# Layer norm with residual on one core: a transfer list of 24 entries in DRAM blocks of 64 rows, in place of 31 entries in blocks of 16

## The chip, the cores and the metric

The kernel runs on one core of a Trainium2 chip. The metric is device time in microseconds (us) of the whole program; lower is better. An ordinary execution and one taken with the profiler differ little. "Span" is the stretch from the first to the last instruction in a profile, some 1.3 us shorter than the device time of the same execution (236.7 against 238.0). Faster or slower needs 2%. A run counts as fast when it lies within 1.5% of the fastest of its kernel. In the views DVE is VectorE, ACT is ScalarE, POOL is GpSimd and SP is SyncE, which issues the transfers; a `q` after a name means the part of the engine that reads its instructions.

## The reference, cut to what matters

```python
# x, residual: (16, 1024, 512) float32; gamma = ones(512), beta = zeros(512)
z = x + residual
mean, var = z.mean(-1), z.var(-1)
out = gamma * (z - mean) / sqrt(var + eps) + beta
```

The 16384 rows of 2048 bytes are spread over 128 partitions, so each partition handles 128 rows of x, of the residual and of the output. Everything is moved once: 67.1 MB in and 33.6 MB out.

## The kernel before: the parts that matter

One list drives all large transfers. A word such as `x16+16` means: load rows 16 to 31 of every partition; `r` is the residual, `o` a store of the result. From here on a "row" is one row in each of the 128 partitions.

```python
BLOCK = 16
Z_ROWS = 64          # x, later the result: room for 64 rows per partition
R_ROWS = 32          # residual, later the sum: room for 32
PLAN = """
x0+8 r0+8 x8+8 r8+8 x16+16 r16+16 x32+16 r32+16 x48+16
o0+16 r48+16 o16+16 x64+16 r64+16 x80+16 o32+16 r80+16
x96+16 r96+16 o48+8 o56+8 r112+8 x112+8 r120+8 x120+8
o64+16 o80+16 o96+16 o112+8 o120+4 o124+4
"""
```

In DRAM, a partition owns `BLOCK` consecutive rows of each stretch of 128 x `BLOCK` rows. A transfer may not cross a block, and becomes one packet per partition:

```python
def dram(t, lo, n):
    b0 = lo - lo % BLOCK
    v = t[P * b0 : P * (b0 + BLOCK), :].rearrange("(p j) d -> p j d", p=P)
    return v[:, lo - b0 : lo - b0 + n, :].rearrange("p a b -> p (a b)")
```

SyncE issues the list in order on one queue, and waits only where a buffer must be free or a result ready:

```python
for kind, lo, n in moves:
    if kind == "x":       # room in zbuf: the stores of the rows 64 earlier have landed
        ...
        move(part(zbuf, Z_ROWS, lo, n), dram(xf, lo, n), sx[...])
    elif kind == "r":     # room in rbuf: rows 32 earlier have passed the reciprocal
        if lo + n > R_ROWS:
            last = (lo + n - R_ROWS) // TURN - 1
            nc.sync.wait_ge(s_rstd[last % Z_TURNS], last // Z_TURNS + 1)
        move(part(rbuf, R_ROWS, lo, n), dram(rf, lo, n), sr[...])
    else:                 # the results are there
        nc.sync.wait_ge(s_out, lo + n)
        move(dram(of, lo, n), part(zbuf, Z_ROWS, lo, n), so[...])
```

(Cuts are marked by "..."; the last branch omits its test for a wait already made.) The computing runs in turns of 4 rows: GpSimd adds, ScalarE takes mean, square sum and root, VectorE the reciprocal and two multiply-adds.

Of the kernel before, what the change touches and what calls it, by code (L numbers as in the profile page):

```python
# [10 lines left out]
ALU = mybir.AluOpType  # L11


BLOCK = 16
Z_ROWS = 64
R_ROWS = 32


PLAN = """
x0+8 r0+8 x8+8 r8+8 x16+16 r16+16 x32+16 r32+16 x48+16  # L20
o0+16 r48+16 o16+16 x64+16 r64+16 x80+16 o32+16 r80+16
x96+16 r96+16 o48+8 o56+8 r112+8 x112+8 r120+8 x120+8
o64+16 o80+16 o96+16 o112+8 o120+4 o124+4
"""


# [12 lines left out]
def kernel(  # L39
# [23 lines left out]
    for word in PLAN.split():  # L63
        kind, (lo, n) = word[0], map(int, word[1:].split("+"))
        assert lo // BLOCK == (lo + n - 1) // BLOCK
        moves.append((kind, lo, n))
# [6 lines left out]
# [5 lines that stand above are left out]
# [235 lines left out]
```

## Time and profile before

| what | number |
|---|---|
| time, three runs | 239.14 us median (238.11 to 239.16) |
| span of the profiled execution | 236.7 us |
| packets of the data queue | 4464 = 31 x 128 data packets + 31 x 16 semaphore writes |
| busy: VectorE, ScalarE, GpSimd | 75%, 78%, 61% |

The page's table of DMA issues shows the sizes. Each line has what is moved, the issuing queue, the count, KB of one transfer and the median us from issue to landing.

```profile
zbuf<-in_x_dram SPq DMA_DIRECT2D x6, 4096.0 KB, 28.9
rbuf<-in_residual_dram SPq DMA_DIRECT2D x6, 4096.0 KB, 21.2
out_dram<-zbuf SPq DMA_DIRECT2D x6, 4096.0 KB, 31.0
...
out_dram<-zbuf SPq DMA_DIRECT2D x2, 1024.0 KB, 10.0
```

A 4096 KB transfer keeps 16 engines for 9.7 us (8 packets of 1213 ns each); here 21 to 31 us pass to its landing. The difference is time spent queued behind others, the sign of a queue that is kept full.

### The profile page before, as it was taken

How to read it: one execution, taken by the hardware profiler on the slowest of the kernel's cores; microseconds unless marked ns; L12 is line 12 of the kernel's file. 1: busy time of each engine (PE TensorE's matmuls, PEld its weight loads, DVE VectorE, ACT ScalarE, POOL GpSimd, SP SyncE). 2: the span in 40 equal slices, each digit the busy share in tenths (PEclk: the TensorE clock that was granted, in tenths of full speed). 3: DMA queues.
4: the chain of work that ended last, by engine and by line, in shares of the span. 5: the costliest groups of instructions: out<-in, count | busy, mean ns of one | idle time of the engine just before them, and what ended most of it. 6: DMA issues, size and time to landing. Idle time of an engine off the chain costs nothing.

```text
span 236.7 us, 1000 instructions
## 1 busy us (share of the span) xinstructions
PE 3.8 (2%) x4; PEld 1.2 (0%) x4; DVE 177.2 (75%) x290; ACT 183.8 (78%) x545; POOL 144.0 (61%) x36
## 2 busy tenths in 40 slices
PE   0600000000000000000000000000000000000000
PEld 0100000000000000000000000000000000000000
DVE  0001999629999999599980999809999999999950
ACT  2019997299999996999909998099999999999600
POOL 0098920999799307993079920899799798800000
DMA  8999999999999999999999999999999999999997
GB/s 310 443 426 432 426 443 443 443 443 443 410 388 443 443 443 432 426 393 432 443 443 443 443 438 421 415 421 432 429 424 435 426 432 440 439 432 443 438 390 324
DMA packets 4469, 100.68 MB, mean 425 GB/s; under 512 B 498, under 2 KB 498, under 8 KB 500
## 3 DMA queue, kind: packets, MB, share of 16 engines
q1 hardware_dynamic: 4464, 100.67, 99.4%
q14 instruction: 1, 0.01, 0.0%
q10 hardware_dynamic: 4, 0.00, 0.0%
HBM read 67.11 MB, written 33.55 MB: 425 GB/s over the span
## 4 chain that ended last, share of the span: by engine, by line
ACT 48%; DMA 35%; POOL 6%; DVE 4%; issue 1%; SPq 1%; ACTq 0%; DVEq 0%; POOLq 0%
DMA rbuf<-in_residual_dram 35%; ACT junk_s L211 25%; ACT junk_m L201 21%; POOL rbuf L178 6%; DVE zbuf L239 3%; ACT std L220 2%; DVE zbuf L253 1%; SPq L140 1%; DVE rstd L247 0%; ACTq L194 0%; DVEq L231 0%; POOLq L175 0%; ACTq L199 0%; ACTq L195 0%
## 5 line engine op out<-in xcount | busy, mean ns | idle before, releaser
L178 POOL TENSOR_TENSOR rbuf<-zbuf,rbuf 128x2048 f32<-128x2048 f32 x32 | 143.7, 4521 | 62.2 <-DMA rbuf<-in_residual_dram 60.0
L239 DVE SCALAR_TENSOR_TENSOR zbuf<-rbuf,nm,gamma_p 128x512 f32<-128x512 f32 x128 | 87.1, 743 | 47.8 <-ACT std L220 47.8
L201 ACT ACTIVATE junk_m<-rbuf 128x512 f32<-128x512 f32 x128 | 74.2, 580 | 34.0 <-POOL rbuf L178 33.7
L211 ACT ACTIVATE junk_s<-rbuf,nm 128x512 f32<-128x512 f32 x128 | 88.8, 694 | 1.0
L253 DVE SCALAR_TENSOR_TENSOR zbuf<-zbuf,rstd,beta_p 128x512 f32<-128x512 f32 x128 | 87.1, 744 | 1.1
L211 ACT ACTIVATION_READ_ACCUMULATOR junk_s<-rbuf,nm 128x1 f32 x128 | 23.9, 187 | 0.0
L201 ACT ACTIVATION_READ_ACCUMULATOR junk_m<-rbuf 128x1 f32 x128 | 23.8, 186 | 0.0
L220 ACT ACTIVATE std<-ssq,eps_t 128x4 f32<-128x4 f32 x32 | 9.5, 297 | 1.0
L247 DVE RECIPROCAL rstd<-std 128x4 f32<-128x4 f32 x32 | 5.5, 171 | 0.0
L192 ACT ACT_TABLE_LOAD x1 | 1.3, 1283 | 2.7 <-PEq L60 2.7
L131 PE MATMUL gamma_p<-gb_row,ones 1*128 1x512 f32 x2 | 2.0, 1122 | 6.6 <-DMA gb_row<-in_gamma_dram 6.6
L131 PE MATMUL beta_p<-gb_row,ones 1*128 1x512 f32 x2 | 1.9, 1056 | 0.0
L126 DVE MEMSET ones<- 1x128 f32 x1 | 0.2, 165 | 2.0 <-PEq L60 2.0
L131 PEld LDWEIGHTS beta_p<-gb_row,ones 1*128 1x128 f32 x2 | 0.7, 332 | 1.0 <-DMA gb_row<-in_beta_dram 0.5
L131 PEld LDWEIGHTS gamma_p<-gb_row,ones 1*128 1x128 f32 x2 | 0.5, 306 | 6.6 <-issue 6.6
L294 POOL MEMSET const-float32-0.0<- 128x1 f32 x1 | 0.1, 98 | 0.2 <-issue 0.2
L294 POOL MEMSET const-bfloat16-1.0<- 128x1 bf16 x1 | 0.1, 101 | 0.0
L294 POOL MEMSET const-uint8-127<- 128x1 uint8 x1 | 0.1, 101 | 0.0
L294 POOL MEMSET const-float32-1.0<- 128x1 f32 x1 | 0.1, 98 | 0.0
L127 DVE MEMSET eps_t<- 128x1 f32 x1 | 0.1, 59 | 0.0
## 6 DMA issues: line engine op xcount, KB each, us to landing
zbuf<-in_x_dram SPq DMA_DIRECT2D x6, 4096.0 KB, 28.9
rbuf<-in_residual_dram SPq DMA_DIRECT2D x6, 4096.0 KB, 21.2
out_dram<-zbuf SPq DMA_DIRECT2D x6, 4096.0 KB, 31.0
zbuf<-in_x_dram SPq DMA_DIRECT2D x4, 2048.0 KB, 14.9
rbuf<-in_residual_dram SPq DMA_DIRECT2D x4, 2048.0 KB, 14.0
out_dram<-zbuf SPq DMA_DIRECT2D x3, 2048.0 KB, 22.5
out_dram<-zbuf SPq DMA_DIRECT2D x2, 1024.0 KB, 10.0
gb_row<-in_gamma_dram ACTq DMA_DIRECT2D x1, 2.0 KB
```

What stands on the lines that cost most here:

```text
L126: nc.vector.memset(ones[:, :], 1.0).then_inc(s_const, 1)
L131: nc.tensor.matmul(dest[:, :], ones[:, :], gb_row[:, k * D : (k + 1) * D], start=True, stop=True).then_inc(s_pe, 1)
L140: i = nc.sync.dma_start(out=out, in_=in_).then_inc(s, 16)
L178: nc.gpsimd.tensor_tensor(out=z, in0=part(zbuf, Z_ROWS, lo, n), in1=z, op=ALU.add).then_inc(s_sum[lo // TURN % R_TURNS], 1)
L192: act.preload_act_table_set("sqrt_and_others")
L201: i = act.activation(out=junk_m[k][:, :], in_=part(rbuf, R_ROWS, r, 1), func=ACT.Identity, scale=-inv_d, accum_out=column(nm, r),)
L211: i = act.activation(out=junk_s[k][:, :], in_=part(rbuf, R_ROWS, r, 1), func=ACT.Square, bias=column(nm, r), accum_out=column(ssq, r),)
L220: act.activation(out=column(std, rows[0], TURN), in_=column(ssq, rows[0], TURN), func=ACT.Sqrt, bias=eps_t[:, 0:1], scale=inv_d,).then_inc ...
L239: dve.scalar_tensor_tensor(out=part(zbuf, Z_ROWS, r, 1), in0=part(rbuf, R_ROWS, r, 1), scalar=column(nm, r), in1=gamma_p[:, :], op0=ALU.ad ...
L247: dve.reciprocal(out=column(rstd, rows[0], TURN), in_=column(std, rows[0], TURN)).then_inc(s_rstd[j], 1)
L253: i = dve.scalar_tensor_tensor(out=z, in0=z, scalar=column(rstd, r), in1=beta_p[:, :], op0=ALU.mult, op1=ALU.add,)
L294: nc = _bacc.Bacc("TRN2", target_bir_lowering=False, num_devices=1)
```

## The change

Its intent: pay the fixed cost of a transfer fewer times. Blocks of 64 rows allow transfers of more than 16 rows (the longest in the list has 28), and the order was chosen with a model of the queue so that it should not run dry.

```diff
-BLOCK = 16
+BLOCK = 64
 PLAN = """
-x0+8 r0+8 x8+8 r8+8 x16+16 r16+16 x32+16 r32+16 x48+16
-o0+16 r48+16 o16+16 x64+16 r64+16 x80+16 o32+16 r80+16
-x96+16 r96+16 o48+8 o56+8 r112+8 x112+8 r120+8 x120+8
-o64+16 o80+16 o96+16 o112+8 o120+4 o124+4
+x0+16 r0+8 r8+24 x16+20 x36+28 r32+16 o0+16 o16+8
+r48+16 x64+24 r64+16 o24+24 r80+16 x88+16 r96+12 o48+16
+x104+8 r108+8 x112+16 r116+12 o64+16 o80+24 o104+16 o120+8
 """
```

No instruction of a computing engine is added, removed or reordered.

## The prediction

> **What bounds the kernel now.** I read the page's rows by slices of time first, then the DMA table, then the queue's own waits, then the chain of waits, and last the transfer records of the trace.
>
> ```profile
> DVE  0001999629999999599980999809999999999950
> ACT  2019997299999996999909998099999999999600
> DMA  8999999999999999999999999999999999999997
> GB/s 310 443 426 432 426 443 443 443 443 443 410 388 443 443 443 432 426 393 432 443 443 443 443 438 421 415 421 432 429 424 435 426 432 440 439 432 443 438 390 324
> ...
> q1 hardware_dynamic: 4464, 100.67, 99.4%
> ```
>
> The DMA row is 9 in 38 of 40 slices, with 8 at the start and 7 at the end. The table says the same: the packets of the one data queue fill 99.4% of the time of all 16 engines. VectorE and ScalarE have visible holes (75% and 78% busy), so neither is full.
>
> The chain of waits seems to contradict this: it gives ACT 48% and DMA 35%.
>
> ```profile
> ACT 48%; DMA 35%; POOL 6%; DVE 4%; issue 1%; SPq 1%; ACTq 0%; DVEq 0%; POOLq 0%
> ```
>
> That chain follows the last store back through the wait that allowed it to be issued. It can't see that the store, once issued, stands behind others in the queue. The queue's own waits show how early the issuing engine runs:
>
> ```profile
> SPq L140 <- DVE rstd L247: 131.6, 7, 38.5
> SPq L140 <- DVE zbuf L253: 50.6, 7, 22.9
> SPq L140 <- DMA out_dram<-zbuf: 32.9, 4, 17.9
> ...
> SPq L164 <- DMA out_dram<-zbuf: 5.5, 2, 3.1
> ```
>
> The issuer waits 215 us at line 140 for buffers and results, yet the DMA engines are never empty: each wait ends while earlier transfers still lie in the queue. So the ScalarE part of the chain is slack, and the end is set by **the sum of the packet times**. In the stretches the view by windows agrees:
>
> ```profile
> 64.00:72.00 8.00, 0.00 (x0) 0.00 (x0) 7.77 (x14) 7.71 (x25) 8.00 (x3) 1.00 0.97 397
> 72.00:180.00 108.00, 0.00 (x0) 0.00 (x0) 89.28 (x146) 92.11 (x275) 72.63 (x17) 1.00 1.00 431
> 180.00:228.00 48.00, 0.00 (x0) 0.00 (x0) 46.03 (x75) 42.12 (x126) 24.16 (x6) 1.00 1.00 431
> ```
>
> The last two columns are DMA share and GB/s: full share at 431 GB/s, through loads, mixtures and pure stores alike.
>
> The records of single packets give the size of that sum. The quickest of each size (and nearly the median): 8192 B 309 ns, 16384 B 611 ns, 32768 B 1213 ns, a 4-byte semaphore write 9 ns. From the last two sizes, 16384 B cost 602 ns, so a row of 2048 B costs 75.25 ns, and 611 - 602 = **9 ns are fixed per packet**. A transfer has one packet per partition, 8 for each of 16 engines, and one semaphore write per engine. So n rows hold every engine for 8 x (75.25 n + 9) + 9 ns = 0.602 n + 0.081 us. For 384 rows (128 of x, 128 of residual, 128 out) in 31 transfers: 231.2 + 31 x 0.081 = 233.7 us. What packets took beyond their quickest adds 1.5 us per engine: 0.7 in the first 4 us, 0.4 around 68 to 72 us (each engine had one slow packet there, up to 1908 ns in place of 1213), the rest scattered. Total 235.2, against 235.16 us of summed packet time per engine in the trace. The remaining 1.5 us of the span of 236.7 are the 1.0 us before the first packet and about 0.5 at the end, where engines stop between 234.9 and 236.1.
>
> **What the Trainium skill says.** Four places, all in "DMA: Bandwidth & Descriptors". "Where 436 GB/s comes from" puts the ceiling at 435 GB/s; the trace agrees: 16 x 2048 B / 75.25 ns = 435.5 GB/s without the fixed part. "Why small descriptors are slow (HBM only)" names a fixed overhead per packet that large ones amortize; this trace shows 9 ns, 0.7% of a 32 KB packet. "Rules for kernel authors" wants at least 1 MiB per DMA; the smallest here is already 1024 KB. "Latency and other measured facts" reports that row pitches in HBM at large powers of two cost bandwidth: 512 KiB gives 207 GB/s per direction where 214 is full, 2 MiB gives 164. The trace of before has only a 32 KiB pitch and shows no loss.
>
> **The change, part by part.**
>
> (1) Fewer transfers. 31 become 24: 7 x 8 = 56 packets fewer per engine at 9 ns = 0.50 us, and 7 semaphore writes at 9 ns = 0.06 us. Sum: **0.57 us** of engine time, all on the path that sets the end, as all engines are full. The bytes stay: 231.2 us remain untouched. Seven issues fewer at 0.33 to 0.5 us each save 2 to 3 us of the issuing engine, which stands waiting most of the time: worth 0.
>
> (2) Block 64. A partition's rows in DRAM now start 128 KiB apart, not 32 KiB, and one packet can be up to 28 rows = 56 KiB. No instruction is added. If 56 KiB goes out as one packet, its cost is the formula's. If it were split in two, the packets saved would partly return: 9 ns x 8 per split transfer, at most 11 transfers above 16 rows or so, under 0.7 us.
>
> (3) The order. This is worth something only if the queue ran dry before, and it did not. It can only lose, if it runs dry now. I walked the new list with measured durations. A transfer ends 0.602 n + 0.081 us after the one before; the first begins at 1.1 and loses 0.7. Data is usable 1.0 us after its last packet (before: residual rows 16 to 31 end by this rule at 40.8; GpSimd's wait for them ended in the trace at 41.37). Four rows take GpSimd 4.54 us, ScalarE 5.76 us (2.46 + 2.94 + 0.30 and gaps in the chain), VectorE 2.85 us to the reciprocal that frees the residual buffer and 5.56 us to the end. An issue takes 1.0 us to its first packet (0.00 to 1.02 in the trace). The rule gives the old list's waits at 43.2, 72.4, 95.5, 121.0, 150.1 us for residual rows 32, 48, 64, 80, 96; the trace has 42.8, 72.0, 95.3, 120.9, 150.1. So it is good to 0.5 us, on the safe side.
>
> One step in full: residual rows 64 to 79 need rows 32 to 47 to have passed the reciprocal. Those end in the queue at 69.7, are usable at 70.7, the first add ends at 75.4 (0.1 for the wait), four ScalarE turns at 98.4, the reciprocal at 101.3. The queue is filled until 108.6. Spare time: 108.6 - 101.3 - 1.0 = 6.3 us. The gated transfers of the new list:
>
> ```
> transfer   may issue  queue filled to  spare us
> r32+16        51.0        60.0          7.9
> r48+16        74.7        84.3          8.6
> x64+24        85.9        94.0          7.1
> r64+16       101.3       108.6          6.3
> r80+16       125.7       132.8          6.1
> x88+16       134.4       142.5          7.1
> r96+12       144.1       152.2          7.1
> x112+16      170.8       179.0          7.2
> o104+16      213.1       220.3          6.2
> o120+8       224.7       230.0          4.4
> ```
>
> The old list by the same rule never has less than about 6 us ahead of the last stores and 3.9 us before the last one. So both lists keep the queue fed, and part 3 is worth 0. The last store is ready at 224.7, before the queue reaches it: the end stays with the packets.
>
> Sum: 236.7 - 0.6 = **236.1 us of span**, and 239.1 - 0.6 = **238.5 us** of measured time.
>
> **The rivals.**
>
> *The pitch costs bandwidth.* For it: the skill's series starts losing at 512 KiB, and engines that run in step would now touch addresses four times further apart. Against it: 128 KiB is a quarter of the smallest pitch that lost anything, and packet times here are so constant (1213 to 1221 ns for the middle nine tenths) that memory behind them seems to have room. With the 3% of the 512 KiB case on all packets the time would be 231 x 1.03 + 7, about 245 us: slower.
>
> *The queue runs dry.* For it: transfers are larger, so each wait asks for more rows, and the last spare is only 4.4 us. Against it: the walk, which misses the old list by under 1 us. A hole would cost its own length, so even a 2 us error in two places leaves it near 239.
>
> *A real gain above 2%.* It would need 4.8 us. Bytes alone at 75.25 ns a row take 231.2 us, plus 2.5 us outside the span (239.1 - 236.7) and 1.0 us before the first packet: 234.7 us with packets, semaphores, slow start and tail all at zero, still above the 234.4 needed. Only a higher byte rate could bring it, and nothing in the diff gives that.
>
> *Noise hides it.* The three times before span 1.05 us, wider than the gain.
>
> **Range and chances.** The centre is 238.5. Below it lie 0.6 us of run spread and the slow packets that may go away (up to 0.7 us): 237.2. Above it lie the same spread, a split of large packets (0.7) and a mild pitch effect (0.2%, 0.5 us): 240.2. Faster by over 2% has 0.02, slower by over 2% (above 243.9, practically only the pitch) 0.03, same 0.95.
>
> **What the new profile would show.** Step 1: 24 x 128 = 3072 data packets and 384 semaphore writes, 3456 on the queue, the queue's share still over 99%, summed packet time per engine near 234.6. Step 2: 32 KiB packets at 1213 ns and 24 rows at 1815 ns (24 x 75.25 + 9); longer ones would mean the pitch costs, and more packets than 3456 a split. Step 3: no slice of the DMA row under 9 but the first and last; issues of residual rows within 1 us of my table. The prediction is wrong if the packets' time per byte changes, if the queue has holes in the middle, or if the part outside the span moves.

## The result, and the profile after

| | before | after |
|---|---|---|
| median of 6 runs of the same rounds | 238.38 us (238.09 to 239.16) | 238.30 us (238.04 to 238.53) |
| ratio of the fast runs | | 0.9989, 95% interval 0.997 to 1.0009 |
| span of the profiled execution | 236.7 us | 236.9 us |

A ratio here is the mean time of one kernel's fast runs over that of the other's of the same rounds, so it is not quite the ratio of the medians quoted. The change is worth 0.3 us give or take 0.5: the same within 2%, and not distinguishable from nothing.

The rows by slices, and the line of the data queue, of the changed kernel:

```profile
DMA  9999999979999999999999899999999999999997
GB/s 354 399 443 473 456 408 415 508 329 465 443 354 443 393 465 423 490 398 398 443 407 506 382 426 431 422 431 441 409 423 451 425 436 429 479 407 431 437 396 329
...
q1 hardware_dynamic: 3456, 100.66, 99.3%
```

The engines are as full as before: 99.3% after 99.4%. The 7 in slice 9 and the 8 in slice 23 are no holes. The view by windows gives the stretch just before each a DMA share above 1 (slice 9: 1.16, then 0.76, then 1.09; slice 23: 1.02 at 124 to 130 us, 0.90 at 130.3 to 136.2), which fits a packet's time being counted where it starts; by the packets' own records all 16 engines are busy at every instant sampled in both slices. In the run below whose 28-row load is cut in two, slice 9 is a 9 again. GB/s jumps between 329 and 508 for the same reason: packets are now up to 56 KB long.

The chain of waits by engine, and the queue's own waits (engine, line, what for, total us, times, longest; `rstd` is the reciprocal that frees the residual buffer, `zbuf` the finished rows):

```profile
DMA 44%; ACT 36%; POOL 8%; DVE 6%; issue 1%; SPq 0%; DVEq 0%
```

```profile
SPq L139 <- DVE rstd L246: 116.6, 7, 47.3
SPq L139 <- DVE zbuf L252: 65.8, 6, 24.4
SPq L139 <- DMA out_dram<-zbuf: 21.5, 2, 13.2
SPq L147 <- DMA out_dram<-zbuf: 11.8, 1, 11.8
```

The chain moved 12 points from ScalarE to other engines, DMA above all, while the time stayed. That is the reading to learn: where the queue is full, as here, this chain says which of several slack paths happened to be followed, not what sets the end. SyncE still waits over 200 us in total, and the engines never notice.

The issue times are in the timeline of the queue (start us, us, engine, line):

```profile
50.63 0.33 SPq L139 DMA_DIRECT2D rbuf<-in_residual_dram  x1
...
74.25 0.34 SPq L139 DMA_DIRECT2D rbuf<-in_residual_dram  x1
86.47 0.34 SPq L139 DMA_DIRECT2D zbuf<-in_x_dram  x1
101.79 0.33 SPq L139 DMA_DIRECT2D rbuf<-in_residual_dram  x1
...
126.19 0.33 SPq L139 DMA_DIRECT2D rbuf<-in_residual_dram  x1
134.75 0.33 SPq L139 DMA_DIRECT2D zbuf<-in_x_dram  x1
144.88 0.33 SPq L139 DMA_DIRECT2D rbuf<-in_residual_dram  x1
```

The prediction's table had 51.0, 74.7, 85.9, 101.3, 125.7, 134.4 and 144.1: right to 0.8 us. Five of the seven came later than the table, so the rule was not "on the safe side" here; 6 us of spare time covered that.

**Where the saving went.** Two stretches of the changed kernel in the view by windows (stretch, busy us and count of PE, PEld, DVE, ACT, POOL, then clock, DMA share, GB/s):

```profile
64.00:72.00 8.00, 0.00 (x0) 0.00 (x0) 7.61 (x13) 7.28 (x22) 0.72 (x1) 1.00 1.00 385
72.00:180.00 108.00, 0.00 (x0) 0.00 (x0) 95.35 (x156) 99.02 (x296) 84.03 (x19) 1.00 1.00 430
```

From 64 to 72 us the DMA share is 1.00 but only 385 GB/s move (0.97 and 397 before); the stretch after it has 430 (431 before). So something is slow just ahead of 72 us. I took the packets' own records, and for each packet the time above the quickest of its size (9, 309, 611, 912, 1213, 1514, 1815, 2116 ns for 4 B and for 8 to 56 KB in steps of 8). Called "excess" from here on, in us per engine (the sum over all packets / 16):

```
                               records    quickest   excess   sum     of the excess: last load
                               per engine times                       ahead of the first store
before                            279      233.66     1.50    235.16   x48+16  0.45
changed kernel                    216      233.11     2.15    235.26   r32+16  0.91
```

The part that the change was made for is there: 233.66 - 233.11 = 0.55 us. (This column is counts times quickest times, so it shows that counts and quickest times came as expected, not that the time was saved.) The excess took it back, 0.65 us. Most sits where the engines turn from loads to stores: the load packet before last, on all 16 engines at once, lasted up to 2171 ns in place of 1213 (in the old list it is the last one, up to 1908). In the old list one load pays this, x48+16, and hardly any later one. In the new list r32+16 paid twice as much, and three later loads ahead of stores (r64, r96, r116) another 0.17, 0.17 and 0.08.

### The profile page after: what moved, and what is told of

The parts are those of the page before. It is cut to its first block, busy times and chain, and to the rows that moved or that the text cites. A ratio compares the mean times of both kernels' runs of the same rounds, so it can differ in the third digit from the quotient of the medians.

```text
span 236.9 us, 985 instructions
## 1 busy us (share of the span) xinstructions
PE 4.1 (2%) x4; PEld 1.0 (0%) x4; DVE 177.2 (75%) x290; ACT 184.1 (78%) x545; POOL 144.1 (61%) x36
## 3 DMA queue, kind: packets, MB, share of 16 engines
q1 hardware_dynamic: 3456, 100.66, 99.3%
## 4 chain that ended last, share of the span: by engine, by line
DMA 44%; ACT 36%; POOL 8%; DVE 6%; issue 1%; SPq 0%; DVEq 0%
DMA rbuf<-in_residual_dram 26%; ACT junk_s L210 19%; DMA zbuf<-in_x_dram 17%; ACT junk_m L200 16%; POOL rbuf L177 8%; DVE zbuf L238 5%; ACT std L219 2%; DVE zbuf L252 1%; DVE rstd L246 0%; SPq L139 0%; DVEq L230 0%
```

## The experiments

Theories: **P**, the wider pitch in DRAM makes the turns costly; **S**, size and order of the transfers do; **C**, chance of one profile. Apart from these I tested the two premises of the prediction: what a packet really costs, and whether the walk of the queue finds holes. All kernels gave correct results. They ran on four chips (the first four runs on one, the next four on a second, three on a third, the last on a fourth), each round with the kernel before in it; its medians there lay between 238.06 and 238.30 us. Times are compared within rounds; an excess comes from one profile of each altered kernel, two of the unaltered ones, and is compared across chips (that of the first comparison is not on record), so that the chip and the scatter of one profile are not excluded as causes of its differences.

**The pitch alone.**

```diff
 # the kernel before
-BLOCK = 16
+BLOCK = 64
```

> The old list of 31 transfers, only the DRAM block raised from 16 to 64 rows (a partition's rows 128 KiB apart in place of 32). Theory P (the pitch makes the last load packets before a run of stores slow): the time that packets take beyond the quickest of their size rises from 1.5 us per engine to about 2.1, with slow packets ahead of the later store runs too (near 90, 128, 167, 196 us), and the time rises by 0.4 to 0.7 us. Rival S (size and order of the new list do it): 1.5 us as before, time within 0.2 us of the kernel before. Rival C (chance of one run): either, without a pattern at the changes from loads to stores.

Measured: 238.32 us, ratio to before 1.0008 (0.9987 to 1.0029). Excess 1.63 us by the scale above, first turn 0.46, one later turn at 0.16 (r48+16). With the old list the first turn is untouched by the pitch, so the pitch alone does not explain the 0.9 us, and the time shows no cost of 128 KiB. Whether pitch and new list together make the turn slow was not tested.

**Twice the pitch again.**

```diff
 # the changed kernel
-BLOCK = 64
+BLOCK = 128
```

> The new list with the DRAM block raised from 64 to 128 rows (256 KiB apart). Theory P: the excess grows further, from 2.15 to 2.5 us or more per engine, and the time by 0.3 us or more over 238.3. Rivals S and C: 2.1 us and 238.3 us, no change.

Measured: 239.47 us (239.02 to 240.45), ratio to before 1.0056 (1.0033 to 1.0079), an interval clear of the changed kernel's (0.997 to 1.0009). Excess 2.65 us in the profiled run, one of the quicker (239.06), of it 1.33 in r32+16 and 0.28 in r96+12. So a pitch effect exists, some 0.6%, but at 256 KiB and not visibly at 128.

**What a packet costs.** The new list, every entry cut into pieces of 4 rows:

```diff
-x0+16 r0+8 r8+24 x16+20 ...
+x0+4 x4+4 x8+4 x12+4 r0+4 r4+4 r8+4 r12+4 ...        # 96 entries in all
```

> The new list with every transfer cut into pieces of 4 rows: 96 transfers in place of 24, packets of 8 KiB, same order and pitch. 72 more transfers put 576 packets and 72 semaphore writes on each engine. Theory R (the records' 9 ns each are all paid): 648 x 9 ns = 5.8 us more, 244.1 us. Rival O (neighbouring packets of an engine overlap by some 3.3 ns, as their records in the trace do, so only 5.7 ns each are paid): 3.7 us more, 242.0 us. Were nothing of it on the path that sets the end: 238.3 us.

Measured: 242.79 us, ratio to before 1.0189 (1.017 to 1.0208). The page still has a full queue:

```profile
DMA  8999999999999999999999999999999999999996
...
q1 hardware_dynamic: 13824, 100.67, 99.8%
```

Against the changed kernel's 238.30 that is 4.5 us for 648 more records per engine, 6.9 ns each, between the two theories. (By the mean end of the 16 engines, 239.15 against 235.80 and 235.47 in two profiles of the changed kernel, it is 5.4 ns. Against the kernel before, of the same rounds, it is 4.5 us for 585 more records, 7.7 ns.) The excess, 2.70 us, is 0.5 to 0.8 above that of the two profiles of the changed kernel, so part of the 4.5 us is no fixed cost of a record. So the records do cost time on the path that sets the end, but not all of their 9 ns; that neighbouring records of an engine overlap by 3 to 4 ns in the traces fits this. For the change's 63 records fewer this gives an estimate of 63 x 5.4 to 7.7 ns = 0.34 to 0.49 us, not 0.57. A surprise: the first turn cost nothing measurable here, on 8 KB packets on both sides.

**A naive merge.** The old list with neighbours merged where blocks of 16 allow it:

```diff
 # the kernel before; the other words unchanged
-x0+8 r0+8 x8+8 r8+8
+x0+16 r0+16
-o48+8 o56+8 r112+8 x112+8 r120+8 x120+8
+o48+16 r112+16 x112+16
-o112+8 o120+4 o124+4
+o112+8 o120+8
```

> The old list with its 8-row and 4-row neighbours merged to 16 rows wherever the block of 16 allows: 25 transfers, pitch 32 KiB kept. The walk of the queue predicts three holes: 3.5 us before residual rows 32 to 47 (near 50 us), 3.5 us before residual rows 112 to 127 (near 180 us) and 1.3 us before the last store. By the walk the time is 243.3 - 235.5 = 7.8 us above the old kernel less 0 for fewer packets (already in the walk): about 246 us. Rival (the order costs nothing, only the number of packets counts): 0.4 us below the kernel before, 237.9 us.

Measured: 247.98 us, ratio 1.0404 (1.0384 to 1.0424): 25 transfers in place of 31, and 9.6 us slower. The rows of the page, and two stretches in the view by windows (stretch, busy us and count of PE, PEld, DVE, ACT, POOL, then clock, DMA share, GB/s):

```profile
DMA  8999999939999999999999999999949999999988
...
q1 hardware_dynamic: 3600, 100.66, 96.3%
```

```profile
50.00:55.00 5.00, 0.00 (x0) 0.00 (x0) 4.96 (x9) 4.97 (x16) 5.00 (x2) 1.00 0.39 105
...
180.00:188.00 8.00, 0.00 (x0) 0.00 (x0) 7.33 (x13) 7.73 (x24) 8.00 (x3) 1.00 0.51 184
```

The holes are where the walk put them, before residual rows 32 to 47 and 112 to 127. Here the roles are exchanged: ScalarE and GpSimd are full in the stretch and the queue waits for them. The walk said 7.8 us in all. By the packets' records the holes were 3.4, 3.5 and 0.9 us, a little less than its 3.5, 3.5 and 1.3. What it did not have came on top: each restart of the idle queue cost 0.7 us of excess, and the first turn after each restart 0.97 and 1.25 us, together 3.2 us more than the old list's one turn of 0.45. (Holes and restarts sum to 11.0 us; the profiled span is 10.1 longer, 246.8 against 236.7. The 54 records fewer per engine explain at most 0.5 of the difference, the rest is not placed.) So the order is worth nothing only as long as it leaves no hole; this list of fewer transfers in the old layout cost 4%. The new blocks and the searched order reach 24 transfers without a hole; a better order of 25 in blocks of 16 was not tried.

**Does the size of the packets at a turn set its cost?** Three edits of the new list, and the changed kernel unaltered:

```diff
 # last 4 load rows ahead of each run of stores on their own
-r32+16 ... r64+16 ... r96+12 ... r116+12
+r32+12 r44+4 ... r64+12 r76+4 ... r96+8 r104+4 ... r116+8 r124+4
 # first 4 store rows on their own
-o0+16 ... o24+24 ... o48+16 ... o64+16
+o0+4 o4+12 ... o24+4 o28+20 ... o48+4 o52+12 ... o64+4 o68+12
 # the 28-row load cut
-x36+28
+x36+12 x48+16
```

> The new list, but the last 4 rows of each of the four loads that stand ahead of a run of stores are a transfer of their own (r32, r64, r96, r116), so that the engines turn from loads to stores on 8 KiB packets; 28 transfers. Theory L (what costs at a change is the load packet in flight, in proportion to its size): the excess of those loads falls from 1.33 us in sum to 0.4 or less; 4 more transfers cost 0.3 us; time 237.7 us. Rival T (the change costs what it costs, whatever the size of the last load): 1.33 stays, time 238.6 us.

> The new list, but the first 4 rows of each of the four runs of stores are a transfer of their own (o0, o24, o48, o64); 28 transfers. Theory L: excess of the loads ahead of them stays at 1.33 us, time 238.6 us. Rival F (the size of the first store packets makes the last loads slow): excess falls to 0.4 us or less, time 237.7 us.

> The new list with its 28-row load (56 KiB packets) cut into x36+12 and x48+16, as the last but one load ahead of the first stores; 25 transfers. Theory B (large packets ahead of the last load make the first change cost 0.9 us in place of the 0.45 us it cost in the old list): the excess of residual rows 32 to 47 falls to 0.5 us, time 238.0 us. Rival: it stays at 0.9 us, time 238.4 us.

> The changed kernel once more, unaltered, on this chip. If the slow packets at the changes from loads to stores are a property of the list, the excess of r32, r64, r96 and r116 comes out near 0.90, 0.17, 0.17 and 0.09 us again; if they are chance, it will be another pattern, and the sum may lie anywhere between 0.4 and 1.4 us.

Measured, in the same rounds, where the kernel before had 238.09 us:

| run | time, us | ratio to before (95%) | first turn, us | r64, r96, r116 |
|---|---|---|---|---|
| last loads cut | 238.59 | 1.0021 (1.0007 to 1.0034) | 0.78 | 0.03, 0.03, 0.05 |
| first stores cut | 238.33 | 1.0007 (0.9994 to 1.0021) | 1.19 | 0.03, 0.02, 0.05 |
| 28-row load cut | 238.25 | 1.0006 (0.9992 to 1.0019) | 0.81 | 0.01, 0.03, 0.03 |
| changed kernel again | 238.07 (one run) | | 0.95 | 0.07, 0.02, 0.03 |

The repeat speaks for C at the later turns: what r64, r96 and r116 had cost in the first profile is mostly gone in the unaltered kernel (in the run with the old start below, r64 and r96 again show 0.09 and 0.15). It also repeats the first turn, 0.91 and 0.95. None of the three theories L, F and B survives; none of the three cuts brings the first turn near 0.45 (in the third, x48+16 took another 0.15), and the first cut is the only one whose time is clear of the kernel before, on the slow side.

**Both sides small, the old start, the old kernel again, and the old list with r32 last.**

```diff
 # new list
-r32+16 o0+16 o16+8
+r32+4 r36+4 r40+4 r44+4 o0+4 o4+4 o8+4 o12+4 o16+4 o20+4
 # new list
-x0+16 r0+8 r8+24
+x0+8 r0+8 x8+8 r8+8 r16+16
 # old list
-r32+16 x48+16 o0+16
+x48+16 r32+16 o0+16
```

> The new list with the last load ahead of the first stores (r32+16) and the first run of stores (o0+16, o16+8) cut into pieces of 4 rows: 10 transfers in place of 3, 31 in all, everything ahead as in the new list. When all 96 transfers had 4 rows the first change from loads to stores cost nothing measurable; with only the last 4 load rows cut it cost 0.78 us, with only the first 4 store rows cut 1.19 us. Theory B2 (both sides small is what takes the cost away): the excess of the last loads falls below 0.2 us; 7 more transfers cost 0.4 us; time 237.7 us. Rival H (the history since the start decides, not the pieces at the change): excess 0.8 us or more, time 238.6 us.

> The new list with the old list's start: x0+16 r0+8 r8+24 become x0+8 r0+8 x8+8 r8+8 r16+16; 26 transfers, the first change from loads to stores untouched. Theory H (the history since the start decides): the excess of r32+16 falls from 0.95 to about the 0.45 us of the old list, time 238.0 us. Rival: it stays at 0.8 to 1.2 us, time 238.4 us.

> The old kernel once more, unaltered. If the cost of the first change belongs to the list, x48+16 shows 0.45 us of excess again (0.446 in the old kernel's trace, 0.461 at the larger pitch) and summed packet time per engine is 235.2 us; if it is chance, another value between 0 and 1.3 us.

> The old list (31 transfers, pitch 32 KiB) with x48+16 and r32+16 exchanged, so that residual rows 32 to 47 are the last load ahead of the first stores, as in the new list; the walk shows no hole. Theory D (which load stands last, the residual or x, decides what the first change costs): excess of r32+16 near 0.95 us in place of the 0.45 to 0.61 us that x48+16 had, time 0.4 us above the kernel before. Rival: it stays at 0.4 to 0.65 us, time as before.

| run | time, us | ratio to before (95%) | first turn, us |
|---|---|---|---|
| both sides in pieces of 4 | 238.50 | 1.0016 (1.0003 to 1.003) | 0.75 |
| old start | 238.11 | 1.0000 (0.9986 to 1.0014) | 0.71 |
| kernel before again | 238.07 (one run) | | 0.61 |
| old list, r32 last | 238.28 | 1.0007 (0.999 to 1.0023) | 0.51 |

Pieces of 4 only around the turn do not repeat what 96 pieces of 4 did. Which load stands last makes no visible difference in the old list. The old start gives the lowest value of the new list, 0.71, so what the engines have done since they started may matter, but it does not reach the old 0.45 to 0.61. Both lists repeat: 0.45, 0.46, 0.51 and 0.61 in four profiles of the old list (original or little altered), 0.71 to 1.19 in seven of the new one at its own pitch. The gap is narrow where the chip was the same: 0.61 against 0.71 and 0.75 in the table above. So the extra cost seems to go with the new list, but **the cause of that difference stays open.**

None of the ten altered kernels beats both kernels; the best is the new list with the old start, ratio 1.0000.

## Why the prediction was right, and which term was off

The class (same) and the range held: 238.3 us against a centre of 238.5. The nearness of the centre flatters the working. The forecast was a saving of 0.6 us, taken from a median of 239.14; with six runs that median is 238.38, from which the same working gives 237.8. Measured was 0.1 us between the medians, 0.3 give or take 0.5 by the ratio.

- **The bound.** Right. The queue's share stayed above 99%, and the experiment with 25 naive transfers showed what time does when it falls to 96.3%.
- **Part 1, fewer transfers, 0.57 us.** Right in count (3456 records on the queue) and in the records' times (233.66 to 233.11), off in size. Two terms fail. A record's 9 ns are not all paid: the experiment with 96 transfers puts them at 5.4 to 7.7, so 0.34 to 0.49 us. And the sum of packet times, forecast at 234.6, came to 235.26 and, in the repeat, 234.97. The step "what packets took beyond their quickest adds 1.5 us" was carried over unchanged; it measured 2.15 and 1.86. The first turn from loads to stores accounts for the part that repeats: on the mean of two profiles each, 0.93 against 0.53, so 0.4 us given back. Saved 0.34 to 0.49, given back 0.4: by this account the net is near nothing. The times, good to 0.5 us, can't check it; the mean end of the engines agrees with it (235.40 and 235.58 us before, 235.80 and 235.47 after).
- **Part 2, block 64.** Right as far as the runs see. No packet was split: 28 rows left as one packet of 57344 bytes in 2116 ns at the median, and 24 rows took 1815 ns, as the formula said. (The list has 6 transfers above 16 rows, not 11; a split of all would have cost 6 x 72 ns = 0.43 us by the prediction's rule, and 11 would have been 0.79, not under 0.7.) The pitch rival is out at 128 KiB (1.0008 alone, with the old list) and real at 256 KiB (1.0056).
- **Part 3, the order.** Right. The issue times that the timeline shows came within 0.8 us of the table, and the same walk foretold the naive list's two large holes. Its sum there, 7.8 us, was too small: the holes were about as long as it said, and the restart costs came on top. Its sign "no slice of the DMA row under 9 but the first and last" did not come out to the letter (slices 9 and 23), though neither is a hole.
- **A real gain above 2%.** None came, but the sum that excluded it was too tight. Its 2.5 us outside the span mixed two executions (and 239.1 - 236.7 is 2.4); within one execution it is 1.3 to 1.4 us (238.0 and 236.7, 238.28 and 236.9). So the floor is 231.2 + 1.4 + 1.0 = 233.6 us, and 2% below 238.38 is 233.6 as well: a gain of 2% would have needed every other cost to vanish.

## What to carry to other kernels

When the records show the DMA engines full from start to end, count what is fixed per packet before regrouping transfers: here it was at most 31 x 0.081 = 2.5 us of 238, and removing under a quarter of it is lost in the run spread. Regrouping is not harmless, though, because the list that left the queue empty twice for 3.5 us and once for 0.9 cost 9.6 us, many times what fewer packets can save; walk the queue with measured durations first. And sum the packets' excess separately from their quickest times, since that is where a saving that "must" be there can be given back.

## What the Trainium skill lacked or had wrong

- "DMA: Bandwidth & Descriptors", "Latency and other measured facts", has no row pitch below 512 KiB. Here 128 KiB alone cost nothing visible (1.0008, 0.9987 to 1.0029), and 256 KiB about 0.6% (1.0056 against 0.9989).
- The same page's "Rules for kernel authors" asks for at least 1 MiB per DMA. Agreed in kind, but at exactly 1 MiB per transfer (96 of 4 rows) a full queue still lost 1.9%, 5.4 to 7.7 ns per record; going from mostly 4 MiB to as much as 7 MiB gained nothing visible (0.9989, 0.997 to 1.0009).
- No page that I read mentions what these records show on a queue that goes from idle to loads and from loads to stores: 0.5 to 0.7 us of slow packets after each start, and 0.4 to 1.3 us at the first turn to stores after it, in every list but the one of 96 small transfers.
